# Output gate multiplied into the last product's weight columns 256 to 512 by VectorE, in place of the sum over those columns

## The chip, the cores and the metric

The kernel runs on one core of one Trainium2 chip. The time is the device time of one execution in microseconds (us). The kernel before was timed in three runs: median 1295.92 us, lowest 1295.3, highest 1296.21. One execution of it was profiled.

## The reference, cut to what matters

One layer of a diffusion block: an input projection feeds two token mixers, whose outputs are merged into M (512 tokens by 2048 channels). The change touches only the end:

```python
y = (g_a * y_a + g_b * y_b) @ w_o        # M @ w_o, 512 x 2048 by 2048 x 2048
new_xs = xs + gate[:, None] * y          # gate: one number per output column
return _rmsnorm(new_xs, final_g)         # per token, over its 2048 columns
```

The gate is a row: it scales a column of the output. A column of the output depends on the same column of `w_o` alone, so `gate * (M @ w_o)` and `M @ (w_o * gate)` are the same thing column by column. All numbers are float32.

## The kernel before

**Seven products.** A large matrix product here is done in groups of 1024 output columns. M is cut into two halves of 256 tokens and two halves of 1024 contraction rows, and the weights into two halves of contraction rows and two chunks of 512 columns. Seven products of sums of such blocks take the place of eight (Winograd's scheme). The last two groups are the output projection: group 8, then group 9 (object `last_group`). Group 9 runs its products in the order P1, Q5, P2, Q6, P7, Q3, Q4. Sums that share a PSUM accumulator add up there: Q5, Q6 and Q3 in "b", P7 and Q4 in "c". The four outputs of group 9 are, by token half and chunk, (0,0) after P2, (1,1) after P7, (0,1) after Q3 and (1,0) after Q4, so the last one written is token half 1, chunk 0. An output has 256 tokens: two blocks of 128, called t=0 and t=1.

**Pieces.** A product takes its weights in four pieces of 256 contraction rows, a tile of 128 partitions by 2 x 512 numbers. float32 products are made out of reduced-precision ones: ScalarE rounds a piece to `whi` (line L179), VectorE writes the rest `wlo` = piece - `whi` (L180), and TensorE does three matmuls (L335, L336, L337), the second of which reads `wlo`. `split_piece` does this; `get` asks for the split of a few pieces ahead of the one that TensorE is about to use. Some of these tiles are printed with the name `s` in place of `whi` and `wlo`, because they lie in other pools.

**The chain of weights.** Sums of weight blocks are kept in four buffers, one for each piece number; the trace calls each of them `R`, and they are R_1331, R_1332, R_1329 and R_1330 for the pieces 0, 1, 2 and 3. P7 needs the buffer minus another block (L273). After that, the last block is added to the buffer by an accumulating DMA that GpSimd issues (L288), and what results is Q4's weight piece. Q4's splits read it.

**Q4 of the last group** (`finish`): 24 matmuls of 512 columns for t=0, added onto the result of P7 in "c"; then, for t=1, 24 matmuls of 256 columns into a bank of their own (columns 0 to 256, `sums[0]`), then 24 more into another (columns 256 to 512, `sums[1]`). P7's part for t=1 is not in these: `prepare`, called before Q3, takes it from Y (the tile of the output (1,0)), multiplies Y by minus the gate, and GpSimd's DMA adds x onto it.

**The end** (`out_done(0, 1)` and `last`). When Q3 is done, output (0,1) is gated and added up (L1824, L1825), and the RMS of token half 0 and its scaling and stores follow. Then `last` multiplies each of Q4's sums by the gate into a temporary (`weigh`, L1906), adds it to Y (`add`, L1907), takes squares, roots and scales, and stores.

**What sets the order.** Each engine runs its instructions in one fixed order. A tile scheduler makes that order when the program is built; in `out_done(0, 1)` and `last` it is written out by hand for VectorE and ScalarE. Each engine then waits, instruction by instruction, for semaphores. GpSimd and SyncE issue the DMAs in the order of their own queues.

Of the kernel before, what the change touches and what calls it, by code (L numbers as in the profile page):

```python
# [13 lines left out]
ALU = mybir.AluOpType  # L14
# [4 lines left out]
P = 128  # L19
# [102 lines left out]
def block_kernel(ctx, tc, xT, ctx_rows, ctx_toks, x, c_row, w_ss, w_gate, vecs, qkg, rope, dft_c, dft_s,  # L122
                 w_start, w_g, w_pab, w_o, final_g, out):
    nc = tc.nc
# [132 lines left out]
    last_split, split_of, in_line = [], [], []  # L257

    look = [1]

    def split_piece(e):
        if e.out is not None or e.kind == "raw":
            return
        raws = [r for _, r in e.raws]
        src = raws.pop(0) if e.stage is None else chain[e.pc]
        for r in raws:
            nc.vector.tensor_tensor(src, src, r, op=ALU.add)
        if e.off:
            with ExitStack() as line:
                if e.key[1] in DIFF_IN_LINE:  # L270

                    line.enter_context(tc.issue_after(split_of[-2][1].ins))
                nc.vector.tensor_tensor(src, chain[e.pc], src, op=ALU.subtract)  # L273
        hi, lo = e.dst() if e.dst else hl_tiles()
        if isinstance(hi, Halves):
            for k in range(2):
                last_split.append(split_from(src[:, 512 * k : 512 * k + 512].rearrange("p (a c) -> p a c", a=2),
                                             hi.parts[k], lo.parts[k]))
        else:
            hi, lo = hi[:, : e.cols], lo[:, : e.cols]  # L280
            with ExitStack() as line:
                if in_line:
                    for i in last_split[-1]:
                        line.enter_context(tc.issue_after(i.ins))
                last_split.append(split_from(src, hi, lo))
        split_of.append(last_split[-1])
        if e.nxt is not None:
            nc.gpsimd.dma_start(chain[e.pc], e.nxt, accum_op=ALU.add)  # L288
        if e.stage == 3:
            left[e.pc] = 0  # L290
        r = lambda t: t if isinstance(t, Halves) else t.rearrange("p (n m) -> p n m", n=e.n)
        e.out = (r(hi), r(lo))
# [732 lines left out]
    class Group:  # L1025
# [113 lines left out]
        def finish(self, a, form):  # L1139

            w = []
            for j in range(8):
                if j % 2 == 0:
                    w.append(get(("Q4", self.g, j // 2)))
                    job()
                    job()
                self.mm(a, form, j, 0, w[j // 2], False, j == 7, cont=True)
            sums = [b[:, 1, :256] for b in a.b]
            for n, o in enumerate(sums):
                for j in range(8):  # L1150
# [660 lines left out]
    def prepare(t, half, j, inner=None):  # L1811

        o[half, j] = t
        if inner is not None:
            nc.vector.tensor_tensor(t[:, 1, :], t[:, 1, :], inner, op=ALU.subtract)
        nc.vector.scalar_tensor_tensor(t, t, -1.0, row(gates, j), op0=ALU.mult, op1=ALU.mult)
        nc.gpsimd.dma_start(t, x[half, j], accum_op=ALU.add)

# [80 lines left out]
    def last(Y, a, sums):  # L1899
# [4 lines left out]
        half = [(slice(0, 256), 0), (slice(256, 512), 4)]  # L1904
        r = [Rms(2), Rms(3)]
        weigh = lambda c, v: nc.vector.tensor_tensor(tmp[:, c], v, gates[0][:, 0, c], op=ALU.mult)  # L1906
        add = lambda t, c: nc.vector.tensor_tensor(Y[:, t, c], tmp[:, c], Y[:, t, c], op=ALU.add)  # L1907
        (c0, _), (c1, _) = half
        with tc.manual_schedule(engines={mybir.EngineType.DVE, mybir.EngineType.Activation}):
            weigh(slice(0, 512), a)  # L1910
            for c, i in half:
                add(0, c)
                squares_of(Y[:, 0, c], 2, i)
            r[0].add()
            r[0].root()
            r[0].turn()
            r[0].scale(3, True)
            weigh(c0, sums[0])
            add(1, c0)
            squares_of(Y[:, 1, c0], 3, 0)  # L1920
            r[0].scale(1)
            r[0].scale(2, True)
            r[0].scale(0)
            r[1].rest()
            weigh(c1, sums[1])
            add(1, c1)
            r[1].finish(Y[:, 1, c1], tmp[:, c1], 4)
            r[1].scale_part(3, half)
            r[1].scale(1)
# [16 lines left out]
    for name in ONE_GROUP:  # L1946
        if name == "Q3":

            nc.scalar.activation(mhalf[:, 8:9], ssq[:, 0, 2:3], ACT.Sqrt)
            prepare(last_group.Y, 1, 0, last_group.acc["c"][:, 1, :])  # L1950
        elif name == "P7":
            prepare(last_group.X, 0, 1)
        if name in ("P7", "Q3"):
# [89 lines left out]
```

## Time and profile before

| what | value |
|---|---|
| median of 3 runs | 1295.92 us (1295.3 to 1296.21) |
| the profiled execution | 1296.19 us, of which the span from its first to its last instruction is 1294.4 us |
| mean granted TensorE clock | 0.995 |
| busy in the span: TensorE matmuls | 1278.3 us, 99% |
| busy in the span: VectorE | 996.9 us, 77% |
| busy in the span: ScalarE | 683.2 us, 53% |
| busy in the span: GpSimd | 168.9 us, 13% |

By stage, for the last products (times are us from the start of the span):

| stretch | what runs on TensorE | length | TensorE busy | VectorE busy | ScalarE busy |
|---|---|---|---|---|---|
| 1241.9 to 1252.8 | Q6 | 10.90 | 10.90 | 10.36 | 5.20 |
| 1252.8 to 1263.7 | P7 | 10.90 | 10.90 | 9.33 | 6.54 |
| 1263.7 to 1274.6 | Q3 | 10.90 | 10.90 | 8.79 | 3.19 |
| 1274.6 to 1286.1 | Q4 | 11.50 | 11.43 | 9.45 | 8.89 |
| 1286.1 to 1294.4 | nothing | 8.30 | 0.00 | 2.82 | 1.81 |

Instructions of one engine overlap a little at their ends, so a back-to-back row of them starts at shorter distances than their durations: a VectorE operation on 128 x 1024 numbers is listed with 1.22 us, and the next one starts 1.13 to 1.14 us after it. In a timeline, the square brackets at the end of a row hold the idle time of the engine before it and what ended that.

### The profile page before, as it was taken

What the parts mean: (1) busy time and instruction counts of PE and PEld (TensorE: products, weight loads), DVE (VectorE), ACT (ScalarE), POOL (GpSimd) and SP (SyncE); (2) the same over time, 40 slices, a digit from 0 to 9 for tenths busy, and PEclk for the clock granted to TensorE, in tenths of its full rate; (3) what the DMA queues carried; (4) which work ended last, traced back from release to release, by engine and by line L of the source; (5) the groups of instructions that cost most, each with busy time, mean ns of one, the idle gap of its engine ahead of it and who ended that gap; (6) DMA issues with size and microseconds to landing.
All of it is one profiled execution on the core that took longest, in us unless ns stands there. A gap on an engine that the chain in (4) does not pass through costs nothing.

```text
span 1294.4 us, 17752 instructions
## 1 busy us (share of the span) xinstructions
PE 1278.3 (99%) x6622; PEld 1052.6 (81%) x6622; DVE 996.9 (77%) x1309; ACT 683.2 (53%) x1075; POOL 168.9 (13%) x222
## 2 busy tenths in 40 slices
PE   8999999999999999999999999999999999999997
PEld 5677888888888888888888888888888888888886
DVE  5767899979688787658686756788898767887676
ACT  5322655545456455443355544666667646464544
POOL 0000011110202111012021010011100212211210
PEclk8999999999999999999999999999999999999999
DMA  9999587888899889977879897578862899998986
GB/s 377 407 367 353 195 227 204 240 237 255 206 307 260 246 281 292 293 193 194 275 200 279 274 235 259 173 238 253 263 180 79 243 249 258 244 209 229 221 207 175
DMA packets 104487, 319.61 MB, mean 247 GB/s; under 512 B 9904, under 2 KB 33072, under 8 KB 100432
## 3 DMA queue, kind: packets, MB, share of 16 engines
q1 hardware_dynamic: 55056, 197.86, 42.4%
q0 software_dynamic: 27024, 98.19, 35.5%
q10 hardware_dynamic: 22320, 22.42, 5.1%
q8 instruction: 52, 0.85, 0.3%
q14 instruction: 35, 0.29, 0.1%
HBM read 283.82 MB, written 34.61 MB: 246 GB/s over the span
## 4 chain that ended last, share of the span: by engine, by line
PE 93%; DVE 2%; ACT 2%; DMA 1%; issue 1%; SPq 0%; ACTq 0%; DVEq 0%
PE banks L335 10%; PE banks L336 10%; PE banks L337 10%; PE x L336 9%; PE x L335 9%; PE x L337 9%; PE y L335 7%; PE y L336 7%; PE y L337 7%; PE banks L1520 2%; PE pd L563 2%; PE pb L335 1%; PE pb L336 1%; PE pb L337 1%; PE pc L335 1%; PE pc L336 1%
## 5 line engine op out<-in xcount | busy, mean ns | idle before, releaser
L179 ACT ACTIVATE whi<-R 128x1024 fp32r<-128x1024 f32 x138 | 145.2, 1058 | 141.1 <-PE banks L337 50.2
L180 DVE TENSOR_TENSOR wlo<-R,whi 128x1024 fp32r<-128x1024 f32 x138 | 167.4, 1220 | 54.0 <-ACT whi L179 53.8
L180 DVE TENSOR_TENSOR wlo<-wr,whi 128x1024 fp32r<-128x1024 f32 (+1 forms) x122 | 147.0, 1211 | 66.3 <-ACT whi L179 66.2
L179 ACT ACTIVATE whi<-wr 128x1024 fp32r<-128x1024 f32 (+1 forms) x122 | 127.3, 1051 | 125.0 <-PE y L337 39.1
L335 PE MATMUL banks<-whi,s 128*128 128x512 f32 (+1 forms) x400 | 157.7, 394 | 0.9 <-DVE ev L1085 0.9
L336 PE MATMUL banks<-wlo,s 128*128 128x512 f32 (+1 forms) x400 | 155.9, 390 | 0.3 <-DVE wlo L180 0.3
L337 PE MATMUL banks<-whi,s 128*128 128x512 f32 (+1 forms) x400 | 155.8, 389 | 0.0
L335 PE MATMUL x<-whi,s 128*128 128x512 f32 x352 | 137.2, 390 | 0.0
L336 PE MATMUL x<-wlo,s 128*128 128x512 f32 x352 | 137.0, 389 | 0.0
L337 PE MATMUL x<-whi,s 128*128 128x512 f32 x352 | 137.0, 389 | 0.0
L335 PE MATMUL y<-whi,s 128*128 128x512 f32 x316 | 123.1, 389 | 0.1
L336 PE MATMUL y<-wlo,s 128*128 128x512 f32 x316 | 123.1, 389 | 0.0
L337 PE MATMUL y<-whi,s 128*128 128x512 f32 x316 | 122.8, 389 | 0.0
L288 POOL DMA_DIRECT2D R<-in_w_g x64 | 55.9, 874 | 413.4 <-DVE wlo L180 243.1
L179 ACT ACTIVATE s<-wr 128x512 fp32r<-128x512 f32 (+2 forms) x93 | 60.3, 677 | 72.6 <-DMA wr<-cf_d 24.9
L180 DVE TENSOR_TENSOR s<-wr,s 128x512 fp32r<-128x512 f32 (+2 forms) x93 | 66.7, 747 | 35.1 <-ACT s L179 34.2
L335 PEld LDWEIGHTS banks<-whi,s 128*128 128x128 f32 x400 | 75.2, 188 | 16.6 <-DVE ev L1085 1.3
L337 PEld LDWEIGHTS banks<-whi,s 128*128 128x128 f32 x400 | 75.1, 188 | 15.2
L336 PEld LDWEIGHTS banks<-wlo,s 128*128 128x128 f32 x400 | 75.3, 188 | 14.2 <-DVE wlo L180 0.7
L335 PEld LDWEIGHTS x<-whi,s 128*128 128x128 f32 x352 | 66.1, 188 | 13.7
L336 PEld LDWEIGHTS x<-wlo,s 128*128 128x128 f32 x352 | 66.1, 188 | 13.7 <-DVE wlo L180 0.2
L337 PEld LDWEIGHTS x<-whi,s 128*128 128x128 f32 x352 | 66.1, 188 | 13.7
(325 smaller groups left out, 2833.1 us busy)
## 6 DMA issues: line engine op xcount, KB each, us to landing
wr<-in_w_g SPq DMA_DIRECT2D x128, 512.0 KB, 5.7
R<-in_w_g POOLq DMA_DIRECT2D x64, 512.0 KB, 7.3
wa<-in_w_ss SPq DMA_DIRECT2D x31, 1024.0 KB, 9.4
R<-in_w_g SPq DMA_DIRECT2D x32, 512.0 KB, 5.8
wr<-in_w_gate SPq DMA_DIRECT2D x32, 512.0 KB, 5.0
wr<-in_w_o SPq DMA_DIRECT2D x24, 512.0 KB, 7.0
R<-in_w_o POOLq DMA_DIRECT2D x24, 512.0 KB, 9.5
wr<-in_w_pab SPq DMA_DIRECT2D x20, 512.0 KB, 5.7
```

What stands on the lines that cost most here:

```text
L179: first = nc.scalar.activation(hi, src, ACT.Copy)
L180: return first, nc.vector.tensor_tensor(lo, src, hi.bitcast(F32), op=ALU.subtract)
L288: nc.gpsimd.dma_start(chain[e.pc], e.nxt, accum_op=ALU.add)
L335: nc.tensor.matmul(o, ah, bh, start=start, stop=False, skip_group_check=cont)
L336: nc.tensor.matmul(o, ah, bl, start=False, stop=False, skip_group_check=cont)
L337: nc.tensor.matmul(o, al, bh, start=False, stop=stop, skip_group_check=cont)
L563: nc.tensor.matmul(acc[32 * j : 32 * j + 32], c2[:, n, :], w[:, k, :], start=n < 4, stop=n >= KK - 4)
L1520: nc.tensor.transpose(tp[:, k * P : (k + 1) * P], p[:, k * P : (k + 1) * P], ident)
```

## The change

Before Q3 runs, the four Q4 pieces of group 9 are entered in a table `by_columns`. When such a piece is split, VectorE first multiplies its columns 256 to 512, for both contraction halves of the piece (128 x 2 x 256 numbers), by the gate's row, in place in the `R` buffer. Q4's sums over these columns then come out gated. So they can no longer be added onto P7's ungated part: Q4's t=0 starts a fresh sum, and `prepare` takes P7's part from Y for both t. At the end, `weigh` is done only for columns 0 to 256; for columns 256 to 512 `add` reads the PSUM sum itself.

```diff
+    by_columns = {}
...
+        if e.key in by_columns:
+            w = src.rearrange("p (k c) -> p k c", k=2)[:, :, 256:]
+            nc.vector.tensor_tensor(w, w, by_columns[e.key].broadcast_to([P, 2, 256]), op=ALU.mult)
         hi, lo = e.dst() if e.dst else hl_tiles()
...
-                self.mm(a, form, j, 0, w[j // 2], False, j == 7, cont=True)
+                self.mm(a, form, j, 0, w[j // 2], j == 0, j == 7)
...
         if inner is not None:
-            nc.vector.tensor_tensor(t[:, 1, :], t[:, 1, :], inner, op=ALU.subtract)
+            for i in range(2):
+                nc.vector.tensor_tensor(t[:, i, :], t[:, i, :], inner[:, i, :], op=ALU.subtract)
...
-        add = lambda t, c: nc.vector.tensor_tensor(Y[:, t, c], tmp[:, c], Y[:, t, c], op=ALU.add)
+        add = lambda t, c, v: nc.vector.tensor_tensor(Y[:, t, c], v, Y[:, t, c], op=ALU.add)
...
-            weigh(slice(0, 512), a)
+            weigh(c0, a[:, c0])
             for c, i in half:
-                add(0, c)
+                add(0, c, a[:, c] if i else tmp[:, c])
...
             weigh(c0, sums[0])
-            add(1, c0)
+            add(1, c0, tmp[:, c0])
...
-            weigh(c1, sums[1])
-            add(1, c1)
+            add(1, c1, sums[1])
...
-            prepare(last_group.Y, 1, 0, last_group.acc["c"][:, 1, :])
+            prepare(last_group.Y, 1, 0, last_group.acc["c"])
+            by_columns.update({("Q4", 9, pc): gates[0][:, 0, None, 256:] for pc in range(4)})
```

The line numbers of the kernel after are 3 to 5 higher: L273 is L274, the new multiply is L277, L1085 is L1089, L1815 and L1816 are L1820 and L1821, L1849 is L1854, L1906 and L1907 are L1911 and L1912. TensorE, ScalarE, GpSimd and SyncE have the same instructions in the same order; VectorE has 1237 in place of 1232. Its order changes at three places, shown here; besides, the `weigh` of t=0 is half as long.

The first place is VectorE while TensorE works on Q6 and P7: the differences for P7 (L273) and the splits (L180) of P7's pieces 0 to 3 (tiles wlo_10304, s_10324, wlo_10342, s_10365) and of Q3's piece 0 (wlo_10370). Before:

```order
L180 TENSOR_TENSOR wlo_10304<-wr_10225,whi_10303 128x1024
L273 TENSOR_TENSOR wr_10261<-R_1329,wr_10261 128x1024
L180 TENSOR_TENSOR s_10324<-wr_10243,s_10323 128x1024
L273 TENSOR_TENSOR wr_10282<-R_1330,wr_10282 128x1024
L180 TENSOR_TENSOR wlo_10342<-wr_10261,whi_10341 128x1024
L180 TENSOR_TENSOR s_10365<-wr_10282,s_10364 128x1024
L1085 TENSOR_TENSOR s_10358<-banks,s_10131 128x1024
L180 TENSOR_TENSOR wlo_10370<-wr_10300,whi_10369 128x1024
L1085 TENSOR_TENSOR s_10207<-s_10358,s_10207 128x1024
L1816 SCALAR_TENSOR_TENSOR s_10131<-s_10131,s_10133 128x1024
```

And now (s_10133 is the gate's row):

```order
L180 TENSOR_TENSOR wlo_10304<-wr_10225,whi_10303 128x1024
L274 TENSOR_TENSOR wr_10261<-R_1329,wr_10261 128x1024
L277 TENSOR_TENSOR R_1331<-R_1331,s_10133 128x2x256
L180 TENSOR_TENSOR s_10324<-wr_10243,s_10323 128x1024
L274 TENSOR_TENSOR wr_10282<-R_1330,wr_10282 128x1024
L180 TENSOR_TENSOR wlo_10342<-wr_10261,whi_10341 128x1024
L277 TENSOR_TENSOR R_1332<-R_1332,s_10133 128x2x256
L1089 TENSOR_TENSOR s_10358<-banks,s_10131 128x1024
L180 TENSOR_TENSOR s_10365<-wr_10282,s_10364 128x1024
L1089 TENSOR_TENSOR s_10207<-s_10358,s_10207 128x1024
L1821 SCALAR_TENSOR_TENSOR s_10131<-s_10131,s_10133 128x1024
L180 TENSOR_TENSOR wlo_10370<-wr_10300,whi_10369 128x1024
```

The multiplies of Q4's pieces 0 and 1 stand between the splits of P7's pieces, and each waits for the accumulating DMA into its buffer; before, nothing on VectorE read those buffers until Q4's own splits.

The second place is VectorE while TensorE works on P7 and Q3: from the split of Q3's piece 3 (wlo_10424) to those of Q4's pieces 0 to 3 (in the rows before, s_10448, s_10452, wlo_10468, wlo_10484). Before:

```order
L180 TENSOR_TENSOR wlo_10424<-wr_10405,whi_10423 128x1024
L1085 TENSOR_TENSOR s_10358<-s_10358,banks 128x512 x2
L1815 TENSOR_TENSOR s_10207<-s_10207,banks 128x512
L1849 TENSOR_TENSOR s_10358<-s_10358,s_10133 128x1024
L1816 SCALAR_TENSOR_TENSOR s_10207<-s_10207,s_10133 128x1024
L180 TENSOR_TENSOR s_10448<-R_1331,s_10447 128x1024
L180 TENSOR_TENSOR s_10452<-R_1332,s_10451 128x1024
L180 TENSOR_TENSOR wlo_10468<-R_1329,whi_10467 128x1024
L180 TENSOR_TENSOR wlo_10484<-R_1330,whi_10483 128x1024
L1824 TENSOR_TENSOR s_10511<-banks,s_10133 128x512
```

And now:

```order
L277 TENSOR_TENSOR R_1329<-R_1329,s_10133 128x2x256
L277 TENSOR_TENSOR R_1330<-R_1330,s_10133 128x2x256
L180 TENSOR_TENSOR wlo_10424<-wr_10405,whi_10423 128x1024
L1089 TENSOR_TENSOR s_10358<-s_10358,banks 128x512 x2
L1820 TENSOR_TENSOR s_10207<-s_10207,banks 128x512
L1854 TENSOR_TENSOR s_10358<-s_10358,s_10133 128x1024
L1820 TENSOR_TENSOR s_10207<-s_10207,banks 128x512
L180 TENSOR_TENSOR s_10450<-R_1331,s_10449 128x1024
L1821 SCALAR_TENSOR_TENSOR s_10207<-s_10207,s_10133 128x1024
L180 TENSOR_TENSOR s_10455<-R_1332,s_10454 128x1024
L180 TENSOR_TENSOR wlo_10472<-R_1329,whi_10471 128x1024
L180 TENSOR_TENSOR wlo_10489<-R_1330,whi_10488 128x1024
```

The multiplies of pieces 2 and 3 stand ahead of Q3's last split, and the second subtraction of P7's part (L1820) ahead of Q4's first; right behind the last row comes L1829, which was L1824.

The third place is the very end on VectorE, the last block of the last output. Before:

```order
L1868 TENSOR_SCALAR r_10621<-r_10621 128x1
L1906 TENSOR_TENSOR s_10619<-banks,s_10133 128x256
L1907 TENSOR_TENSOR s_10207<-s_10619,s_10207 128x256
L1872 SCALAR_TENSOR_TENSOR s_10619,ssq<-s_10207 128x256
L1887 RECIPROCAL r_10621<-r_10621 128x1
```

And now:

```order
L1873 TENSOR_SCALAR r_10626<-r_10626 128x1
L1912 TENSOR_TENSOR s_10207<-banks,s_10207 128x256
L1877 SCALAR_TENSOR_TENSOR s_10624,ssq<-s_10207 128x256
L1892 RECIPROCAL r_10626<-r_10626 128x1
```

One step, the multiplication of the last sum by the gate, has gone from the row.

## The prediction

> **What bounds the kernel now.** I read the page's totals first, then the chain of waits over the end, then VectorE's, GpSimd's and TensorE's timelines from 1240 us on.
>
> ```profile
> span 1294.4 us, 17752 instructions
> PE 1278.3 (99%) x6622; PEld 1052.6 (81%) x6622; DVE 996.9 (77%) x1309; ACT 683.2 (53%) x1075; POOL 168.9 (13%) x222
> ```
>
> TensorE is the bound almost throughout, so VectorE work costs nothing as long as TensorE gets its pieces in time. The end differs. The chain of waits there:
>
> ```profile
> 1273.86 0.24 PE banks L337
> 1274.13 0.70 DVE s L1824
> 1275.63 0.73 ACT s L1799 x2
> 1279.28 1.32 ACT s L1894 x2
> 1282.55 0.52 ACT s L1799 x2
> 1286.15 0.35 DVE s L1906
> 1286.52 0.43 DVE s L1907
> 1288.88 0.61 ACT s L1894
> ```
>
> From Q3's end the chain leaves TensorE for good: it runs over VectorE's L1824 and ScalarE's squares and scales to the last store. Whatever delays L1824 delays the end one for one, although Q4's matmuls still run. VectorE reaches L1824 early today:
>
> ```profile
> 1263.34 1.28 DVE L1085 TENSOR_TENSOR s<-s,banks 128x512 f32<-128x512 f32 x2
> 1264.53 0.68 DVE L1815 TENSOR_TENSOR s<-s,banks 128x512 f32<-128x512 f32 x1
> 1265.13 1.22 DVE L1849 TENSOR_TENSOR s<-s,s 128x1024 f32<-128x1024 f32 x1
> 1269.67 2.35 DVE L180 TENSOR_TENSOR wlo<-R,whi 128x1024 fp32r<-128x1024 f32 x2
> 1274.13 0.69 DVE L1824 TENSOR_TENSOR s<-banks,s 128x512 f32<-128x512 f32 x1 [2.10 <-PE banks L337]
> ```
>
> It is idle for 2.10 us ahead of L1824, and for 1.49 ahead of Q3's last split:
>
> ```profile
> 1262.19 1.22 DVE L180 TENSOR_TENSOR wlo<-wr,whi 128x1024 fp32r<-128x1024 f32 x1 [1.49 <-ACT whi L179]
> ```
>
> These 3.6 us are the cover for everything that is added before L1824; once they are used up, L1824 is late, and with it the end.
>
> **What it removes.** The last sum's `weigh` goes: its row and the next in VectorE's timeline are
>
> ```profile
> 1286.07 0.42 DVE L1906 TENSOR_TENSOR s<-banks,s 128x256 f32<-128x256 f32 x1
> 1286.52 0.42 DVE L1907 TENSOR_TENSOR s<-s,s 128x256 f32<-128x256 f32 x1
> ```
>
> so 1286.52 - 1286.07 = **0.45 us** leaves the chain. (The `add` now reads PSUM; L1906 does so too, and takes the same 0.42.) The `weigh` of t=0 shrinks from 512 to 256 columns, but there the chain runs through ScalarE (its squares at 1282.55), so that is worth nothing.
>
> **What it adds.** Four multiplies of 512 numbers per partition, and one more subtraction of 512. None like the multiply is in the trace; the rows nearest in size are the 128x512 ones above, which follow one another at 0.60 us (1264.53 to 1265.13), and a bound above is a 128x1024 at 1.14 (1253.64 to 1254.78 in a fence below). I take 0.60, since the count of elements is the same, and keep 1.14 for the range; below 0.60 nothing points. Five times 0.60 is 3.0 us of work, which the cover of 3.6 would hide, and which would cost its 3.0 in full without it.
>
> The larger cost is a **wait**. Each multiply waits for the accumulating transfer into its buffer, and VectorE's queue stands still behind it: P7's splits, Q3's, then Q4's, for which TensorE waits in turn. GpSimd issues these transfers at
>
> ```profile
> 1243.33 0.85 POOL L288 DMA_DIRECT2D R<-in_w_o  x1 [18.75 <-ACT whi L179]
> 1244.22 0.85 POOL L1851 DMA_DIRECT2D s<-in_x  x1
> 1246.73 0.85 POOL L288 DMA_DIRECT2D R<-in_w_o  x1 [1.65 <-ACT whi L179]
> 1249.00 0.85 POOL L288 DMA_DIRECT2D R<-in_w_o  x1 [1.42 <-ACT s L179]
> 1251.54 0.86 POOL L288 DMA_DIRECT2D R<-in_w_o  x1 [1.69 <-ACT whi L179]
> ```
>
> and the table of DMA issues, asked for each alone, gives the time to landing of the first, second and third (the fourth has the third's):
>
> ```profile
> R<-in_w_o POOLq DMA_DIRECT2D x1, 512.0 KB, 5.6
> ...
> R<-in_w_o POOLq DMA_DIRECT2D x1, 512.0 KB, 9.9
> ...
> R<-in_w_o POOLq DMA_DIRECT2D x1, 512.0 KB, 11.3
> ```
>
> So the buffers are ready at 1248.9, 1256.6, 1260.3 and 1262.8. VectorE's clock over the first place:
>
> ```profile
> 1247.25 1.22 DVE L273 TENSOR_TENSOR wr<-R,wr 128x1024 f32<-128x1024 f32 x1
> 1248.65 1.22 DVE L180 TENSOR_TENSOR s<-wr,s 128x1024 fp32r<-128x1024 f32 x1 [0.18 <-ACT s L179]
> 1249.79 1.22 DVE L273 TENSOR_TENSOR wr<-R,wr 128x1024 f32<-128x1024 f32 x1
> 1253.64 1.22 DVE L1085 TENSOR_TENSOR s<-banks,s 128x1024 f32<-128x1024 f32 x1
> 1254.78 1.21 DVE L180 TENSOR_TENSOR wlo<-wr,whi 128x1024 fp32r<-128x1024 f32 x1
> ```
>
> Multiply 0 is reached at 1247.25 + 1.14 = 1248.4 and starts at 1249.0. Behind it stand a split, a difference and a split, 3 x 1.14, so multiply 1 is reached at 1249.6 + 3.4 = 1253.0. Its buffer lands at 1256.6: VectorE stands for **3.6 us**. From 1256.6 to L1829 (L1824 before) the order then has, back to back: three multiplies, 1.8; four operations of 512 (L1089 twice, L1820 twice), 2.4; fourteen of 1024 (nine splits: P7's piece 3, Q3's four, Q4's four; and two L1089, two L1821 and L1854) at 1.135, 15.9. Sum 20.1, so L1829 starts at 1276.7. The multiplies 2 and 3 are reached at about 1265.2 and 1265.8, after their landings, and wait for nothing, also with the fourth transfer issued 0.95 us later, behind the shifted difference (1249.79 becomes 1250.74).
>
> Does TensorE get its pieces? It uses them from
>
> ```profile
> 1260.90 0.39 PE L335 MATMUL banks<-s,s 128*128 128x512 f32 x1
> 1263.69 0.40 PE L335 MATMUL banks<-whi,s 128*128 128x512 f32 x1
> 1274.61 0.39 PE L335 MATMUL banks<-s,s 128*128 128x512 f32 x1
> ```
>
> (P7's piece 3, Q3's piece 0, Q4's piece 0). The splits now end at 1256.6 + 0.6 + 1.14 + 1.22 = 1259.6; three operations later at 1263.0; and, with L180 for Q4's piece 0 started at 1271.1, at 1272.3. Each is in time, by 1.3, 0.7 to 0.9 and 2.3 us; Q4 follows at 1.39 us a piece, slower than VectorE's 1.14. TensorE doesn't idle, by a narrow margin. Y's own DMA (issued at 1267.92 before, 7.3 us to landing)
>
> ```profile
> 1267.92 0.87 POOL L1817 DMA_DIRECT2D s<-in_x  x1 [0.16 <-issue]
> s<-in_x POOLq DMA_DIRECT2D x1, 512.0 KB, 7.3
> ```
>
> moves with its L1821 (now 1272.2) to an issue near 1274.0 and a landing by 1281.3; its reader comes at 1283.4. Covered.
>
> **Sum.** L1824 moves from 1274.13 to 1276.74: +2.61. The end loses 0.45. Together **+2.2 us** on the profiled execution, 1296.19 + 2.16 = 1298.35. That execution is 0.27 above the median of the runs, so for the median I say **1298.1 us**, 0.17% slower. For this kernel 0.2% (2.6 us, 1293.3 to 1298.5) is about what a measurement tells from no change; the forecast lies just inside.
>
> With 1.14 a multiply, three behind the wait cost 1.6 more: 1299.7.
>
> **Rivals.**
>
> *The transfers land early, and the multiplies are hidden.* If multiply 1 finds its buffer ready at 1253.0, L1829 is reached at 1273.1 by the same 20.1 us, before Q3's end lets it start. Only the 0.45 is left: 1295.5. It needs a landing below 1254.1 (1274.13 less 20.1), under 7.4 us from issue. For it: the first transfer took 5.6, the least of all. Against it: the second took 9.9, with the x transfer and a weight load beside it, and neither is touched by the change.
>
> The Trainium skill ("DMA: Bandwidth & Descriptors", Anatomy of one DMA — SWDGE path) has a fit that speaks for this rival: 2.0 us plus bytes over 436 GB/s. For 512 KB that is an estimate of 3.2 us, a landing at 1249.9, and no wait at all. The rows above, 5.6 to 11.3, don't agree, since several transfers share the engines here; by the page the time would be the rival's 1295.5.
>
> *The landing slips, and TensorE starves.* Every microsecond that R_1332 lands later goes to the end in full, and from a landing past about 1257.4 Q3's piece 0 is late too (margin 0.7 to 0.9), so TensorE idles as well. At the 11.3 us of the next two transfers it lands at 1258.0: L1829 at 1278.1, +3.6 in all, 1299.5, clearly slower. For it: the queue is full at that time, and the landings of this line between 1190 and 1270 us spread
>
> ```profile
> DMA to landing us min/median/max: 5.6/9.9/16.0
> ```
>
> Against it: what goes before that transfer in its queue is unchanged. At 16.0 it would be 1304.
>
> *The fourth transfer is the one that holds.* It is issued later than before, and multiply 3 stands ahead of Q3's last split. It decides from a landing after 1265.8, 13.3 us from an issue at 1252.5. At 16.0 us VectorE stands 2.7 longer: 1301.0.
>
> **Chances and range.** The forecast as worked out 0.58; landing slips 0.20; multiplies hidden 0.14; fourth transfer 0.06; something that none of these holds, with a gain beyond 0.2%, 0.02. The forecast's own spread is about 1 us either way, by the landing and the length of the multiply, and the bound at +2.6 us cuts through it: some 0.37 of its 0.58 lies within 0.2%, 0.21 above. The hidden case is within 0.2%, the slipped and the fourth transfer above. That gives faster 0.02, same 0.51, slower 0.47. The range runs from the hidden case, 1295.5, to the fourth transfer's price, 1301.0, with the dear multiplies inside.
>
> **What would show it.** In VectorE's timeline of the changed kernel: idle ahead of the second L277 of about 3.6 us, ended by a DMA, the first with 0.6, the other two with none; L277 at 0.68 us long; L1829 with no idle time and a start near 1276.7; Q4's first matmul still at 1274.6 and TensorE without a gap at 1263.7; the last `add` 0.45 us closer to its predecessor. The prediction is wrong if the second L277 starts by 1254, if TensorE waits for `wlo` in P7 or Q3, or if the chain at the end comes from Q4's matmuls rather than from L1829.

## The result and the profile after

| | median | range | runs |
|---|---|---|---|
| before, timed beside it | 1296.09 us | 1295.24 to 1299.21 | 16 |
| after | 1298.56 us | 1296.82 to 1300.45 | 16 |

The ratio of the runs is **1.0015**, 95% interval [1.0008, 1.0022]: slower by 1.0 to 2.9 us. The profiled execution of the changed kernel took 1299.42 us. Its page has a longer span, and VectorE busy for 2.3 us more in it:

```profile
span 1297.7 us, 17751 instructions
PE 1278.9 (99%) x6622; PEld 1052.0 (81%) x6622; DVE 999.2 (77%) x1313; ACT 682.8 (53%) x1075; POOL 168.8 (13%) x222
```

By the page VectorE has 4 instructions more (1309 to 1313): four multiplies and one subtraction more, and one `weigh` less. The section on the change counts 5.

The spans of two executions are not to be compared as they stand: 3.3 us lie between them (1297.7 against 1294.4), but this execution is late before the change begins. The last row of VectorE's timeline that no edit has touched is the third difference, R_1329's (L273 before, L274 now): it started at 1247.25 before, and at 1248.44 here. These 1.19 us come from upstream: a pause that TensorE makes in both kernels at about 814 us ends at 813.80 before, and at 815.06 here. Everything below is therefore counted from that row on. VectorE's timeline of the changed kernel from there (start, length, and in brackets the idle time before it and what ended that):

```profile
1248.44 1.22 DVE L274 TENSOR_TENSOR wr<-R,wr 128x1024 f32<-128x1024 f32 x1
1250.07 0.69 DVE L277 TENSOR_TENSOR R<-R,s 128x512 f32<-128x512 f32 x1 [0.41 <-DMA R<-in_w_o]
...
1252.95 1.22 DVE L180 TENSOR_TENSOR wlo<-wr,whi 128x1024 fp32r<-128x1024 f32 x1
1257.75 0.69 DVE L277 TENSOR_TENSOR R<-R,s 128x512 f32<-128x512 f32 x1 [3.58 <-DMA R<-in_w_o]
1258.36 1.22 DVE L1089 TENSOR_TENSOR s<-banks,s 128x1024 f32<-128x1024 f32 x1
...
1262.89 2.35 DVE L180 TENSOR_TENSOR wlo<-wr,whi 128x1024 fp32r<-128x1024 f32 x2
1265.16 1.22 DVE L180 TENSOR_TENSOR s<-wr,s 128x1024 fp32r<-128x1024 f32 x1
1266.30 1.29 DVE L277 TENSOR_TENSOR R<-R,s 128x512 f32<-128x512 f32 x2
...
1275.58 2.35 DVE L180 TENSOR_TENSOR wlo<-R,whi 128x1024 fp32r<-128x1024 f32 x2
1277.85 0.68 DVE L1829 TENSOR_TENSOR s<-banks,s 128x512 f32<-128x512 f32 x1
```

The second multiply has a bracket of 3.58 us, ended by the accumulating DMA; from there to L1829 no row has one. The brackets that stood ahead of Q3's last split and of L1824 before (1.49 and 2.10) are gone. L1829 starts 29.41 us after the third difference, L1824 did so after 26.88: **2.53 us late**. The end comes 49.3 us after it (1297.7 - 1248.44), before 47.15 (1294.4 - 1247.25): **2.1 us late**.

The chain of waits over the end, in order of time:

```profile
1247.92 9.81 DMA R<-in_w_o
1257.75 0.69 DVE R L277
1258.44 1.13 DVE s L1089
...
1277.93 0.61 DVE s L1829
1278.57 0.70 DVE s L1830
1279.34 0.73 ACT s L1803 x2
```

Before, it left TensorE at Q3's end and went straight to L1824. Now it leaves for a transfer, at 1247.92, and runs through VectorE's whole queue from the second multiply to L1829.

TensorE is not held up. Its row by stretch (length; TensorE, weight load, VectorE, ScalarE, GpSimd busy; granted clock; DMA) shows it busy all the time from P7 to Q4's start, at full clock:

```profile
1255.00:1276.00 21.00, 21.00 (x94) 17.30 (x93) 18.25 (x20) 8.91 (x12) 2.61 (x3) 1.00 0.63 132
```

And the very end, VectorE's last block, before and now without the multiplication by the gate:

```profile
1286.00 0.15 DVE L1868 TENSOR_SCALAR r<-r 128x1 f32<-128x1 f32 x1
...
1286.98 0.42 DVE L1872 SCALAR_TENSOR_TENSOR s<-s 128x256 f32<-128x256 f32 x1
```

```profile
1289.71 0.15 DVE L1873 TENSOR_SCALAR r<-r 128x1 f32<-128x1 f32 x1
1289.78 0.41 DVE L1912 TENSOR_TENSOR s<-banks,s 128x256 f32<-128x256 f32 x1
1290.23 0.42 DVE L1877 SCALAR_TENSOR_TENSOR s<-s 128x256 f32<-128x256 f32 x1
```

From the scalar step to the sum's square it is 0.52 us now (1289.71 to 1290.23); before it was 0.98 (L1868 at 1286.00, L1872 at 1286.98).

### The profile page after: what moved, and what is told of

Its sections match the earlier page's. It is cut to its first block, busy times and chain, and to the rows that moved or that the text cites. A ratio compares the mean times of both kernels' runs of the same rounds, so it can differ in the third digit from the quotient of the medians.

```text
span 1297.7 us, 17751 instructions
## 1 busy us (share of the span) xinstructions
PE 1278.9 (99%) x6622; PEld 1052.0 (81%) x6622; DVE 999.2 (77%) x1313; ACT 682.8 (53%) x1075; POOL 168.8 (13%) x222
## 4 chain that ended last, share of the span: by engine, by line
PE 90%; DMA 4%; DVE 3%; ACT 1%; issue 1%; SPq 0%; ACTq 0%; DVEq 0%; POOLq 0%
PE banks L339 9%; PE banks L340 9%; PE banks L341 9%; PE x L340 9%; PE x L341 9%; PE x L339 9%; PE y L340 8%; PE y L341 8%; PE y L339 8%; PE banks L1524 2%; PE pd L567 2%; PE pb L339 1%; PE pb L340 1%; PE pb L341 1%; DMA wr<-in_w_start 1%
## 5 line engine op out<-in xcount | busy, mean ns | idle before, releaser
L180 DVE TENSOR_TENSOR wlo<-R,whi 128x1024 fp32r<-128x1024 f32 x138 | 167.4, 1221 | 51.9 <-ACT whi L179 51.5
L180 DVE TENSOR_TENSOR wlo<-wr,whi 128x1024 fp32r<-128x1024 f32 (+1 forms) x122 | 147.0, 1212 | 64.4 <-ACT whi L179 64.2
L180 DVE TENSOR_TENSOR s<-wr,s 128x512 fp32r<-128x512 f32 (+2 forms) x93 | 66.8, 749 | 36.0 <-ACT s L179 35.1
```

Of the source, the lines that this page charges most:

```text
L180: return first, nc.vector.tensor_tensor(lo, src, hi.bitcast(F32), op=ALU.subtract)
```

## The experiments

The theory, W in the expectations: the end is late because VectorE's queue stands behind the second multiply's wait for R_1332. Its rivals there are L, that the multiplies' own work is what costs, and U, that one of the other edits does. W had to be made more exact on the way (e10). All ten kernels were timed beside the kernel before. The table gathers their profiled executions; "third difference" is the start of the row explained above, and the two distances are from there to L1824 (or its counterpart) and to the end of the span, with the difference from the kernel before.

| run | third difference | to L1824 | to the end | timed ratio [95% interval] |
|---|---|---|---|---|
| before | 1247.25 | 26.88 | 47.2 | |
| after | 1248.44 | 29.41, +2.53 | 49.3, +2.1 | 1.0015 [1.0008, 1.0022] |
| e1_after_again | 1250.23 | 29.62, +2.74 | 49.5, +2.3 | 1.002 [1.0011, 1.0028] |
| e2_no_wait | 1248.01 | 26.87, -0.01 | 46.7, -0.5 | 0.9997 [0.9989, 1.0006] |
| e3_late | 1247.46 | 26.97, +0.09 | 46.7, -0.4 | 1.0003 [0.9994, 1.0012] |
| e4_wait_alone | 1247.35 | 28.83, +1.95 | 48.7, +1.5 | 1.0018 [1.0009, 1.0027] |
| e5_swap | 1246.60 | 33.28, +6.40 | 53.1, +5.9 | 1.0048 [1.0035, 1.006] |
| e6_gpsimd | 1246.71 | 27.95, +1.07 | 47.8, +0.6 | 1.0005 [0.9996, 1.0013] |
| e7_no_gate | 1246.99 | 26.88, 0.00 | 46.7, -0.4 | 0.9998 [0.9989, 1.0007] |
| e8_fresh | 1247.98 | 26.88, 0.00 | 47.1, 0.0 | 0.9997 [0.9988, 1.0005] |
| e9_x_behind | 1249.05 | 27.61, +0.73 | 47.4, +0.3 | 0.9999 [0.999, 1.0008] |
| e10_wait_same_place | 1248.48 | 27.78, +0.90 | 47.6, +0.4 | 1.0001 [0.999, 1.0011] |

**The change again (e1).** The kernel after, without an edit.

> The changed kernel once more, on the same chip as the next three. Theory W (the second multiply waits for the transfer into its buffer, VectorE stands still, and L1829 and the end are late by what the idle time ahead of L1829 doesn't cover): 2 to 3 us over the kernel before, a ratio of 1.0017, idle time of 3 to 4 us ahead of the second L277, L1829 some 2 us after Q4's first matmul. Rival L (the five added VectorE operations, 3.0 us, are the cost by their length): the same time. Rival U (the loss comes from ahead of the place of the change): a ratio that varies, and L1829 at the same distance from Q4's first matmul as before, -0.5 us.

It took 1298.41 us (1297.51 to 1301.44), and VectorE shows the same wait:

```profile
1259.75 0.69 DVE L277 TENSOR_TENSOR R<-R,s 128x512 f32<-128x512 f32 x1 [3.65 <-DMA R<-in_w_o]
...
1279.85 0.68 DVE L1829 TENSOR_TENSOR s<-banks,s 128x512 f32<-128x512 f32 x1
```

The loss and its place repeat, in an execution that is 3 us later upstream than the profiled one of the kernel before. Its lateness has one main place: TensorE pauses twice at about 531 us, for 0.61 and 1.62 us, and runs at a granted clock of 0.51 from 533.0 to 536.4. That makes about 3.9 us, an estimate from the pauses and half of the 3.4 us.

**The work without the wait (e2).** The multiplies stand at the same places of VectorE's order and are as large, but work on a spare tile that no DMA writes.

```diff
-            w = src.rearrange("p (k c) -> p k c", k=2)[:, :, 256:]
-            nc.vector.tensor_tensor(w, w, by_columns[e.key].broadcast_to([P, 2, 256]), op=ALU.mult)
+            g = by_columns[e.key].broadcast_to([P, 2, 256])
+            with tc.issue_after(split_of[(-8, -7, -4, -5)[e.key[2]]][1].ins):
+                nc.vector.tensor_tensor(spare[0].rearrange("p (k c) -> p k c", k=2)[:, :, 256:], g, g, op=ALU.mult)
```

> The four multiplies stand at the same places in VectorE's order and have the same size, but read the gate's row alone and write a spare tile, so that they wait for no transfer; the gate on columns 256 to 512 of the last output is left out. Theory W: L1829's counterpart is reached before Q3's end, the end moves by the saved step alone, -0.45 us against before, a ratio of 0.9997 (0.9990 to 1.0004). Rival L: the work is all there, so 2 to 3 us slower than before, 1.0017.

1295.68 us (1295.11 to 1296.56). In VectorE's timeline the last two multiplies and the row after Q4's splits:

```profile
1261.82 1.41 DVE L278 TENSOR_TENSOR s<-s 128x512 f32<-128x512 f32 x2
...
1274.88 0.69 DVE L1830 TENSOR_TENSOR s<-banks,s 128x512 f32<-128x512 f32 x1 [1.32 <-PE banks L342]
```

L1830 waits for TensorE again, by 1.32 us: all the added work fits under the cover, with that much left. L, by itself, falls. What is left is more than the 0.6 us that a cover of 3.6 and 3.0 us of work would leave. In the kernel before, VectorE has idle time ahead of P7's splits too, 0.18 us in the row at 1248.65 that the prediction shows, and 0.36 in this one:

```profile
1251.37 1.22 DVE L180 TENSOR_TENSOR wlo<-wr,whi 128x1024 fp32r<-128x1024 f32 x1 [0.36 <-ACT whi L179]
```

So the cover is 4.1 us by these brackets, and about 4.3 by this run (3.0 + 1.32).

**The wait without the work (e4).** The multiplies keep their waits, but are cut to 2 columns of each half. The order changes at one place: the second multiply now stands one split earlier.

```diff
-            w = src.rearrange("p (k c) -> p k c", k=2)[:, :, 256:]
-            nc.vector.tensor_tensor(w, w, by_columns[e.key].broadcast_to([P, 2, 256]), op=ALU.mult)
+            w = src.rearrange("p (k c) -> p k c", k=2)[:, :, 510:]
+            nc.vector.tensor_tensor(w, w, by_columns[e.key][:, :, 254:].broadcast_to([P, 2, 2]), op=ALU.mult)
```

> The multiplies cut to two columns of each contraction half (128x2x2 numbers), so that the waits stay and the work goes; the gate on the other 254 of the columns 256 to 512 of the last output is left out. The second multiply now stands ahead of the split of P7's piece 2. Theory W: idle time of 4 to 5 us ahead of it; behind it fifteen operations of 1024 (17.0 us) and four of 512 (2.4) make L1829 start near 1276.3 in the clock of the profile before, 2.2 late, less 0.45: +1.8 us, 1.0014. Rival L: 0.6 us of added work is left, hidden: -0.45 us, 0.9997.

1298.24 us (1297.15 to 1299.42). VectorE's timeline:

```profile
1256.53 0.17 DVE L277 TENSOR_TENSOR R<-R,s 128x4 f32<-128x4 f32 x1 [5.13 <-DMA R<-in_w_o]
...
1276.18 0.68 DVE L1829 TENSOR_TENSOR s<-banks,s 128x512 f32<-128x512 f32 x1
```

With nearly no work, the queue reaches the second multiply earlier and waits longer, 5.13 us, and the timed runs show the whole loss. That looked like W. But the distances tell more: from the second multiply to L1829 it is 19.65 us here (1276.18 - 1256.53) and 20.10 in the change. Three short multiplies should have taken 3 x 0.52 = 1.6 off; one row took 1.14 of that back, since in this kernel the split of P7's piece 2 stands behind the wait, and in the change ahead of it. So e4 took work away behind the wait and put other work there; e10 undoes the second.

**The wait with little work behind it, in the change's order (e10).** The split stays ahead of the second multiply; that and the two later ones are cut to 2 columns. The first multiply, ahead of the wait, and the second subtraction, behind it, keep their size.

```diff
-            w = src.rearrange("p (k c) -> p k c", k=2)[:, :, 256:]
-            nc.vector.tensor_tensor(w, w, by_columns[e.key].broadcast_to([P, 2, 256]), op=ALU.mult)
+            n = 256 if e.key[2] == 0 else 2
+            w = src.rearrange("p (k c) -> p k c", k=2)[:, :, 512 - n :]
+            with tc.issue_after(split_of[(-8, -7, -4, -5)[e.key[2]]][1].ins):
+                nc.vector.tensor_tensor(w, w, by_columns[e.key][:, :, 256 - n :].broadcast_to([P, 2, n]), op=ALU.mult)
```

> As e4, but in the order of the change: there P7's piece 2 was split behind the waiting multiply, which put 1.14 us more behind the wait; here that split stands ahead of it, as in the change. The first multiply has its full size, the other three are cut to 2 columns of the 256, so Q4's gate on the other 254 columns of pieces 1 to 3 is left out. The wait for R_1332 is the change's, 3.6 us. Theory W as so far told (the wait costs the end its length by itself): L1831 about 2.5 us late, ratio 1.0015 to 1.002. Theory C (what counts is the landing plus what stands behind it: the wait alone about uses up the idle time there was, and the work behind it, three multiplies and the subtraction, counts on top): 20.1 less 3 x 0.52 is 18.5 us behind the landing, L1831 about 0.9 us later than in the kernel before, the end 0.4 us later, ratio 1.0003 (0.9995 to 1.001).

1297.12 us (1295.44 to 1299.08), against 1296.5 beside it. VectorE's timeline:

```profile
1257.75 0.17 DVE L279 TENSOR_TENSOR R<-R,s 128x4 f32<-128x4 f32 x1 [3.56 <-DMA R<-in_w_o]
1257.83 1.22 DVE L180 TENSOR_TENSOR s<-wr,s 128x1024 fp32r<-128x1024 f32 x1
...
1276.26 0.68 DVE L1831 TENSOR_TENSOR s<-banks,s 128x512 f32<-128x512 f32 x1
```

The wait is the change's, 3.56 us, and yet L1831 is only 0.90 us late, as theory C has it: 18.51 us behind the landing in place of 20.10. W as it was told, a wait that costs its length, falls. The exact form is a sum: **the landing, plus all that VectorE has to do behind it, against the moment at which Q3's end lets L1829 start**. The 0.90 us are not the wait's alone: the second subtraction (0.60) and the three short multiplies (0.08 for the first, 1257.75 to 1257.83, and 0.15 for the other two) also stand behind the landing. Without them L1831 would be 0.07 us late, an estimate from these rows: the landing by itself just uses up the idle time. The work alone (e2) is hidden. In the change both draw on the same idle time, and the 2.4 us of added work behind the landing (three multiplies of 0.60 and the subtraction) count almost in full, which gives the 2.53. A kernel with the landing and no added work at all was not run. In the five traces where this one wait decides, the time from the landing to L1829 is what the rows behind it add up to, to 0.1 us: 20.10 in the change and in e1, 19.65 in e4, 18.51 here, 20.10 in e5 below.

**The multiplies where their buffers have landed (e3).** All four are kept, and stand behind Q3's last two splits.

```diff
-            w = src.rearrange("p (k c) -> p k c", k=2)[:, :, 256:]
-            nc.vector.tensor_tensor(w, w, by_columns[e.key].broadcast_to([P, 2, 256]), op=ALU.mult)
+            if e.key[2] == 0:
+                for q in range(4):
+                    w = chain[(e.pc + q) % 4].rearrange("p (k c) -> p k c", k=2)[:, :, 256:]
+                    with tc.issue_after(split_of[-2 if q < 3 else -1][1].ins):
+                        nc.vector.tensor_tensor(w, w, by_columns[e.key].broadcast_to([P, 2, 256]), op=ALU.mult)
```

> The same multiplies on the same buffers, but the first three queued behind the split of Q3's piece 2 and the fourth behind that of Q3's piece 3 or later, when their transfers have landed. Theory W: three multiplies fill idle time ahead of Q3's last split, VectorE reaches L1829's counterpart near 1273.4, some 0.8 us before Q3's end: -0.45 us against before, 0.9997 (0.9990 to 1.0004). Rival L: 2 to 3 us slower than before, 1.0017, since the same work is done.

1296.12 us (1294.99 to 1299.09). In the execution that was profiled, VectorE's timeline has

```profile
1260.91 1.91 DVE L280 TENSOR_TENSOR R<-R,s 128x512 f32<-128x512 f32 x3
1263.48 1.22 DVE L180 TENSOR_TENSOR wlo<-wr,whi 128x1024 fp32r<-128x1024 f32 x1 [0.65 <-ACT whi L179]
...
1274.43 0.68 DVE L1832 TENSOR_TENSOR s<-banks,s 128x512 f32<-128x512 f32 x1
```

No multiply waits for a DMA, and L1832 comes 0.09 us later than L1824 did. It has no idle time left, though: the 0.65 ahead of the split is a weight load of Q3 that was late here, after which ScalarE's timeline shows

```profile
1262.38 1.06 ACT L179 ACTIVATE whi<-wr 128x1024 fp32r<-128x1024 f32 x1 [2.65 <-DMA wr<-in_w_o]
```

So the change costs nothing that can be measured if its multiplies are put behind the landings; in this execution, with that load late, the cover is used up, and any further delay would show.

**A longer wait (e5).** The multiplies of R_1332 and R_1329 change places, so that the second one waits for a transfer that lands later.

```diff
-            w = src.rearrange("p (k c) -> p k c", k=2)[:, :, 256:]
-            nc.vector.tensor_tensor(w, w, by_columns[e.key].broadcast_to([P, 2, 256]), op=ALU.mult)
+            if e.key[2] == 0:
+                for q, n in ((0, 8), (2, 6), (1, 2), (3, 2)):
+                    w = chain[(e.pc + q) % 4].rearrange("p (k c) -> p k c", k=2)[:, :, 256:]
+                    with tc.issue_after(split_of[-n][1].ins):
+                        nc.vector.tensor_tensor(w, w, by_columns[e.key].broadcast_to([P, 2, 256]), op=ALU.mult)
```

> The multiplies of R_1332 (Q4's piece 1) and R_1329 (piece 2) change places, nothing else: the second multiply now waits for the third transfer, which in the profile before lands 3.7 us later (1260.3 in place of 1256.6); the multiply of R_1332 waits for nothing. Theory W (VectorE's queue stands behind the wait, and the end moves by the whole of it): idle ahead of the second multiply of about 7.3 us; the last split of P7 then ends at about 1263.3, 2.4 us after TensorE wants it, and Q3's first about 0.6 late on top, so TensorE idles some 3 us; L1832 (L1829 in the change) starts 3.7 us later than in the change, about 6.3 us later than before; less 0.45 this is +5.8 us on the kernel before, about 1301.8, ratio 1.0045. Rival L (what costs is the multiply itself, on its operands, wherever its wait is): same as the change, ratio 1.0015 to 1.002. Rival S (the wait was already spent as far as the end can see, and the rest of it lies under TensorE's work): ratio at most 1.0025.

1302.38 us (1300.46 to 1304.65, 5 runs). VectorE's and then TensorE's timeline:

```profile
1259.78 0.69 DVE L280 TENSOR_TENSOR R<-R,s 128x512 f32<-128x512 f32 x1 [7.25 <-DMA R<-in_w_o]
...
1279.88 0.68 DVE L1832 TENSOR_TENSOR s<-banks,s 128x512 f32<-128x512 f32 x1
```

```profile
1262.79 0.50 PE L343 MATMUL banks<-s,s 128*128 128x512 f32 x1 [2.16 <-DVE s L180]
```

A wait that is 3.7 us longer (7.25 against 3.58) makes L1832 3.9 us later than in the change (+6.40 against +2.53), and the end 3.8. The landing itself is 3.9 us later too, if it is counted from the third difference (13.18 us against 9.31), so it goes through one for one. S, that the rest lies under TensorE's work, falls: once the idle time is gone, the landing counts in full, with the same 20.10 us behind it (1279.88 - 1259.78). TensorE now starves for 2.16 us, as the prediction's rival of a slipped landing said it would from a landing past 1257.4. The expectation was some 3, with a second pause at Q3's first piece, which doesn't come. The pause has an echo that was not expected: by stretches, with the granted clock third from the end,

```profile
1260.20:1262.80 2.60, 0.44 (x3) 0.02 (x2) 2.60 (x4) 2.00 (x2) 0.00 (x0) 1.00 0.21 39
1262.80:1263.60 0.80, 0.80 (x4) 0.67 (x5) 0.80 (x1) 0.00 (x0) 0.00 (x0) 1.00 0.00 0
1263.60:1266.90 3.30, 3.30 (x9) 2.60 (x8) 3.30 (x4) 0.00 (x0) 0.86 (x1) 0.51 0.04 4
1266.90:1270.00 3.10, 3.10 (x14) 2.51 (x13) 3.10 (x5) 0.90 (x1) 0.00 (x0) 0.97 0.96 156
```

the clock falls to 0.51 for 3.3 us after the pause, and 9 matmuls are done there where 14 are done in the next 3.1, so TensorE comes to Q3 later as well. The end doesn't pay for it here, since VectorE's queue is later still.

**The parts beside the multiplies (e7, e8).** One kernel is the change without the multiplies; the other is the kernel before with the fresh sum and the second subtraction alone.

```diff
-            by_columns.update({("Q4", 9, pc): gates[0][:, 0, None, 256:] for pc in range(4)})
```

> No multiply at all; the last output's columns 256 to 512 leave out the gate on Q4's part. All other edits of the change stay (fresh sum for t=0, second subtraction, short and missing weigh). Theory W: the edits beside the multiplies cost nothing, L1828 right after Q3's end, only the 0.45 us is won: about 1295.6, ratio 0.9997 (0.999 to 1.0005). Rival U (the subtraction, the fresh sum or the later Y transfer cost): ratio above 1.0005, towards 1.0015.

```diff
-                self.mm(a, form, j, 0, w[j // 2], False, j == 7, cont=True)
+                self.mm(a, form, j, 0, w[j // 2], j == 0, j == 7)
...
-            nc.vector.tensor_tensor(t[:, 1, :], t[:, 1, :], inner, op=ALU.subtract)
+            for i in range(2):
+                nc.vector.tensor_tensor(t[:, i, :], t[:, i, :], inner[:, i, :], op=ALU.subtract)
```

> The kernel before with two parts of the change only: Q4's t=0 starts a fresh sum, and P7's part is taken off Y for both t (one subtraction more, 0.6 us, in VectorE's idle time before L1824). No multiply into weights, all weighs as before; the outputs are the reference's. Theory W: ratio 1.0000 (0.9993 to 1.0007), 0.45 us above the run without the multiplies at most. Rival U: ratio 1.001 or more.

1295.65 us (1294.5 to 1296.98) and 1295.48 us (1294.74 to 1297.44). The rows after Q4's splits, of e7 and then of e8:

```profile
1273.87 0.69 DVE L1829 TENSOR_TENSOR s<-banks,s 128x512 f32<-128x512 f32 x1 [1.49 <-PE banks L341]
```

```profile
1274.86 0.69 DVE L1825 TENSOR_TENSOR s<-banks,s 128x512 f32<-128x512 f32 x1 [1.51 <-PE banks L337]
```

Both still wait for TensorE, by 0.6 us less than before: the subtraction. U falls. The two differ by the 0.45 us of the last weigh in their traces (46.7 and 47.1 to the end); the timed ratios can't resolve that.

**The multiplies on GpSimd (e6).** This was meant to beat both kernels: GpSimd multiplies behind its last accumulating DMA, and VectorE's queue holds no wait.

```diff
-            w = src.rearrange("p (k c) -> p k c", k=2)[:, :, 256:]
-            nc.vector.tensor_tensor(w, w, by_columns[e.key].broadcast_to([P, 2, 256]), op=ALU.mult)
+            if e.key[2] == 0:
+                for q in range(4):
+                    w = chain[(e.pc + q) % 4].rearrange("p (k c) -> p k c", k=2)[:, :, 256:]
+                    with tc.issue_after(last_add[0].ins):
+                        nc.gpsimd.tensor_tensor(w, w, by_columns[e.key].broadcast_to([P, 2, 256]), op=ALU.mult)
...
-            nc.gpsimd.dma_start(chain[e.pc], e.nxt, accum_op=ALU.add)
+            last_add[0] = nc.gpsimd.dma_start(chain[e.pc], e.nxt, accum_op=ALU.add)
```

> All four multiplies move from VectorE to GpSimd, behind the issue of the last accumulating transfer; the outputs are the reference's. VectorE's order no longer holds a wait for these transfers. Theory W: L1832 starts where L1824 did before, right after Q3's end, and only the 0.45 us of the last weigh is left: about 1295.6, ratio 0.9997 (0.999 to 1.0005), if GpSimd is done with R_1331 before VectorE's first split of Q4 at about 1267.4 in the profile before, and with the others 1.1 us apart after that. How long GpSimd takes for 128x512 no row shows (it does no arithmetic in this kernel). At up to about 1.9 us each the four are done one after the other by their landings (1248.9, 1256.6, 1260.3, 1262.8) and nobody waits; at 4 us each the last is done at about 1269 to 1270 and still in time for the fourth split at 1270.8; beyond that Q4's splits are late and the gain turns into a loss. The x transfers behind the multiplies in GpSimd's queue are issued later, the last one at or after 1264.5: if one lands after 1275 the end is late by as much. Rival L (the work or another use of the buffers costs, on any engine): ratio 1.001 or more.

1296.92 us (1294.57 to 1297.89). The multiplies take 1.5 to 2.2 us each and are all in time, but L1832 is 1.07 us late and has no idle time before it. GpSimd's and VectorE's timelines say why:

```profile
1251.56 1.64 POOL L280 TENSOR_TENSOR R<-R,s 128x512 f32<-128x512 f32 x1
1256.67 2.17 POOL L280 TENSOR_TENSOR R<-R,s 128x512 f32<-128x512 f32 x1 [3.47 <-DMA R<-in_w_o]
```

```profile
1251.96 2.32 DVE L180 TENSOR_TENSOR s<-wr,s 128x1024 fp32r<-128x1024 f32 x1
...
1257.61 2.31 DVE L1824 SCALAR_TENSOR_TENSOR s<-s,s 128x1024 f32<-128x1024 f32 x1
...
1274.66 0.68 DVE L1832 TENSOR_TENSOR s<-banks,s 128x512 f32<-128x512 f32 x1
```

The VectorE operation that starts during a multiply of GpSimd is listed with 2.31 or 2.32 us in place of 1.22, and ends 1.08 us after GpSimd's (1251.56 + 1.64 = 1253.20, 1251.96 + 2.32 = 1254.28; 1258.84 and 1259.92). The other two multiplies show the same. So each costs VectorE 1.1 us, more than the 0.60 of doing it itself. The Trainium skill ("SBUF — State Buffer", Who interferes with whom) says that a VectorE instruction with two SBUF inputs contends with a GpSimd instruction that reads SBUF, and calls the ports that they share an exclusive lock. These rows agree with it. So the gain that was expected of this place was eaten by the time that VectorE lost beside GpSimd's multiplies, 4.4 us in all, and not by the work as such.

**The x transfer behind R_1332's (e9).** Why is R_1332 so late? Its transfer follows an x transfer in GpSimd's queue. Here the change keeps VectorE's order, and that x transfer is issued right behind it.

```diff
-            nc.gpsimd.dma_start(chain[e.pc], e.nxt, accum_op=ALU.add)
+            last_add = nc.gpsimd.dma_start(chain[e.pc], e.nxt, accum_op=ALU.add)
+            if late_x and e.pc == 3:
+                with tc.issue_after(last_add.ins):
+                    late_x.pop()()
...
-        nc.gpsimd.dma_start(t, x[half, j], accum_op=ALU.add)
-        jobs.extend([lambda: None] * max(0, 5 - len(jobs)) + [lambda: finish_chunk(half, j)])
+        def add_x():
+            nc.gpsimd.dma_start(t, x[half, j], accum_op=ALU.add)
+            jobs.extend([lambda: None] * max(0, 5 - len(jobs)) + [lambda: finish_chunk(half, j)])
+        (late_x.append if (half, j) == (0, 0) else lambda f: f())(add_x)
```

> The change as it is, with one DMA moved: the x transfer that GpSimd issues between the transfers into R_1331 and R_1332 (s<-in_x, 512 KB) now goes right behind the one into R_1332. VectorE's order and the outputs are those of the change. Theory Q (the wait of the second multiply is as long as it is because that x transfer is ahead of R_1332's and takes its share of the engines): R_1332 lands about 2 us sooner (512 KB at the 251 to 257 GB/s that the core moved there), the second multiply waits about 1.5 us in place of 3.6, L1832 starts at most 0.5 us later than in the kernel before, and with the 0.45 us of the last weigh the ratio is about 1.0000 (0.9995 to 1.0008). Rival N (the transfer is slow for the weight loads on SyncE's queue, the x transfer had landed or shares nothing): idle of 3.3 to 3.7 us as in the change, ratio 1.0015 to 1.002. The second shows the prediction's hidden case to be out of reach by this order of the queue.

1296.14 us (1295.2 to 1298.25). The transfer into R_1332, issued at 1248.53, in the table of DMA issues, with its time to landing; in the changed kernel the same row ends in 9.8:

```profile
R<-in_w_o POOLq DMA_DIRECT2D x1, 512.0 KB, 7.2
```

And VectorE's second and fourth multiply and L1832:

```profile
1255.80 0.69 DVE L277 TENSOR_TENSOR R<-R,s 128x512 f32<-128x512 f32 x1 [0.84 <-DMA R<-in_w_o]
...
1265.71 0.69 DVE L277 TENSOR_TENSOR R<-R,s 128x512 f32<-128x512 f32 x1 [0.68 <-DMA R<-in_w_o]
...
1276.66 0.68 DVE L1832 TENSOR_TENSOR s<-banks,s 128x512 f32<-128x512 f32 x1
```

It lands 2.6 us sooner, and the wait shrinks from 3.58 to 0.84 us. That is theory Q, with more gained than the 2 us that it expected; N falls. The fourth transfer is later in turn (issued at 1254.35, used at 1265.7), and its multiply waits for 0.68 us. With the 20.10 us behind the second multiply that gives 20.78 of the 20.86 from 1255.80 to 1276.66, and it is most of the 0.73 that L1832 is still late.

No kernel beats the one before by what can be measured: all that the change can win is the 0.45 us of the last weigh, 0.03%.

## Why the prediction was right

- **The bound.** It took the end to be set by the chain that starts at L1824, and every delay of that row to count in full. In the eleven traces of edited kernels the end moves by L1824's delay less 0.4 to 0.5 us wherever the last weigh is gone: +2.53 gives +2.1, +6.40 gives +5.9, 0.00 gives -0.4. Where it is kept (e8), 0.00 gives 0.0.
- **What is removed.** 0.45 us was forecast; e7, which has that and no multiplies, ends 0.4 earlier.
- **The added work.** The prediction said that its 3.0 us would be hidden by the cover of 3.6 and cost in full without it: e2 (hidden, with 1.32 left) and e10 (1.6 us of it taken out from behind the wait, L1831 1.63 sooner than in the change) show both. The cover itself was read too small, as it left out the short idle times ahead of P7's splits: e2 shows about 4.3. The sum of the forecast starts at the landing and doesn't use it. A multiply was priced at 0.60: 1257.75 to 1258.36 is 0.61, and the two together are listed with 1.29. The dear multiplies fall.
- **The wait.** 3.6 us ahead of the second L277: 3.58 and 3.65. It rests on the landing of one transfer in one trace, 9.9 us. The changed kernel's two profiled executions had 9.8 and 10.0, but the other eight with this order of the queue have 9.7 to 11.5 (11.5 in e3), so that the closeness is in part luck: the prediction counts each microsecond of a later landing in full. That the first would wait 0.6 and the other two not at all: 0.41 and 0.55 for the first, and none for the others.
- **The sum behind it.** 20.1 us from the second multiply to L1829: 1257.75 to 1277.85 is 20.10, and e10 and e4 show that it is this sum, with the rows as they stand behind the landing, that sets L1829. L1829 was forecast at 1276.74, that is 29.49 after the third difference; it came after 29.41.
- **TensorE.** No idle time was forecast from P7 to Q4's start, by narrow margins, and none is there. e5 shows that the margin was real: with a later landing TensorE starves.
- **The fourth transfer.** It was issued later, as forecast, took 10.4 us and landed at 1263.96, 2.9 us before its multiply was reached. In e9, where VectorE gets there sooner and the transfer takes 11.3, the multiply waits.
- **Y's DMA.** Forecast near 1274.0 with a landing by 1281.3. It was issued at 1274.97, that is 1273.8 without the 1.19 us from upstream, and took 6.1 us; its delay reached nobody.
- **The rivals.** The hidden multiplies needed a landing within 7.4 us, and it took 9.8. The estimate of 3.2 us by the Trainium skill's fit ("DMA: Bandwidth & Descriptors", Anatomy of one DMA — SWDGE (gpsimd) path) was not reached by this transfer, which took 7.2 even without the x transfer ahead. The prediction named that transfer, beside a weight load, as what speaks against this rival; e9 shows that it alone makes 2.6 us.

The forecast of 2.16 us compares with 2.1 in the profiled execution and 1.9 (1.0 to 2.9) by the ratio, and the forecast median of 1298.1 with 1298.56. The bound of 0.2% lies inside that interval, as it lay inside the forecast's own spread: which side of it this kernel is on, the runs don't settle. The absolute time of the profiled execution, 1299.42 us against 1298.35, was missed by the 1.19 us from upstream, which has nothing to do with the change.

One step was looser than its number. The prediction called the wait "the larger cost" of the two. In its sum they were 3.6 us and 3.0 against one cover. With the change's order the work alone costs nothing (e2), and the wait with 0.83 us of work behind it costs 0.90 (e10), so that the wait alone would cost next to nothing too, by the estimate above. Neither is the cause without the other.

## What to carry to other kernels

Where work with a wait is added to a queue that runs in order, add up the landing and every row that stands behind it, and compare that with when the last of them was due: idle time that hides the work alone, and by the estimate here about hides the wait alone, doesn't hide both (2.5 us late). The queue ahead of the awaited transfer is part of that price (one DMA moved behind it took 2.6 us off), and moving the work to another engine is not free either, where that engine blocks the first one for longer than the work took. To see 2 us in 1300, count from the last instruction that the change can't have touched, not from the start of the span.

## What was not expected of the hardware

- **A half clock after a short pause.** TensorE idled for 2.16 us in e5, and ran at a granted clock of 0.51 for 3.3 us from 0.8 us after the pause on. The Trainium skill ("TensorE: Matmul & The Clock Gate", Why this matters for your kernels) advises against pauses of more than some 3 us; here a shorter one was followed by the half clock, and the measurement decides. In e1 the same came after two pauses with one matmul between them, 0.61 and 1.62 us. Single pauses of 1.33 us in e9 (to 613.68) and of 1.41 in e10 (to 614.05) were not followed by it: the granted clock is 1.00 in the next 4 us. Where between these the limit lies, no run here shows.
- **VectorE blocked by GpSimd.** Four of four VectorE operations that began during a GpSimd multiply lost 1.1 us each (e6).
- **Drift upstream.** The third difference, which no edit of VectorE's order comes before, started between 1246.60 and 1250.23 in the twelve profiled executions: 3.6 us, more than the whole effect that was to be explained. The latest is e1's, with its pauses and half clock at 531 to 536 us.
